# Both parts of an operand form as one 512-column moving operand in a seven-product feed-forward input projection

## The chip, the core and the metric

The kernel runs on one core of a Trainium2 chip. The metric is the device time of one execution in microseconds (us), as the median over several executions. The engines are named as the profile names them: PE is TensorE's matmul side and PEld its weight loads, DVE is VectorE, ACT is ScalarE, POOL is GpSimd, SP is SyncE, which here only issues DMAs.

## The reference

One layer of a causal decoder: a mixer sublayer, a memory cross-attention sublayer, a SwiGLU feed-forward sublayer and a final norm, for 512 tokens of width 1024. The change lies in the first half of the feed-forward sublayer:

```python
D_MODEL = 1024; SEQ = 512; FFN_HIDDEN = 2816

def rms_norm(x, g):
    xf = x.astype(jnp.float32)
    var = jnp.mean(xf * xf, axis=-1, keepdims=True)
    return (xf * lax.rsqrt(var + EPS) * g.astype(jnp.float32)).astype(x.dtype)

# ... mixer and memory sublayers leave the residual stream x ...
hf = rms_norm(x, norm_ffn[l])
gate, up = jnp.split(hf @ w_ffn_in[l], 2, axis=-1)      # (512, 1024) @ (1024, 5632)
x = x + (jax.nn.silu(gate) * up) @ w_ffn_out[l]
# final: rms_norm(x, norm_final)
```

All arrays are float32.

## The kernel before

Activations lie transposed: model dimension on the 128 partitions, the 512 tokens along the free dimension. A float32 operand is not multiplied as one number: it is split into a rounded part ("hi", made by an ACT cast to fp32r) and the rest ("lo", made by a DVE subtract), and a product is the sum of three matmuls, hi·hi, hi·lo and lo·hi.

The feed-forward input is computed in blocks. The hidden width 2816 makes NF = 22 blocks of 128 gate rows and 128 up rows. In each block m the product of a 2x2 arrangement of weights (gate and up rows by even and odd 128-row chunks of the model dimension) with a 2x2 arrangement of activations (even and odd chunks by two halves of HS = 256 tokens) is made from seven products instead of eight. `forms_of` builds the seven activation forms for each of the KP = 4 pairs of chunks; each is 256 columns wide and is split into hi and lo. The weight forms come per block: two are loaded as they are (`wg`), two come out of a DMA that adds to what is already in the tile (`ws`, first loaded by SP at L763, then added to by POOL's DMA at L768), one is loaded as it is (`a22`, L767), and two are sums made by an engine (`s2`, L779). Each weight form is then cast and subtracted (`ffn_form`, L792, L793, L801, L802).

`product(ps, m, i)` issues product i: for each of the four chunk pairs three matmuls of 256 columns (L811), 12 in all, and 84 per block. They go into the left half of a PSUM bank. A block uses three banks: z collects products 0, 3, 4 and 5 as a running sum, v takes product 1, y takes product 2 and then 6. `reads` and `second` copy or add what the running sums hold after certain products (ACT copies at L831, DVE adds at L833, L836, L841), `evict` scales the gate by the norm factor (L848, DVE), takes silu (L850, ACT) and multiplies with the negated up half (L855, DVE), which gives the block's activation `act`.

The order around it is written out by hand. `uses` lists all products; in the steady part a block is the seven uses (m,3), (m+1,0), (m,4), (m+1,1), (m,5), (m+1,2), (m,6). For use n the loop issues its matmuls, its reads, then the weight form of use n + AHEAD (6 ahead), then the raw weights of use n + 8, then the norm and eviction steps of other blocks. On PE, ACT and DVE instructions stand in exactly that order (`manual_schedule`); POOL and SP are left to the scheduler and carry in this stage only the DMA issues (POOL also made one sum ahead of the loop). Weight tiles come from rotating buffers, so a load waits until the form made from the tile's previous content is done. The last stage, the output projection (matmuls at L155 to L157 into `f`), begins when the loop ends.

Of the kernel before, what the change touches and what calls it, by code (L numbers as in the profile page):

```python
# [40 lines left out]
def hybrid_layer(ctx: ExitStack, tc: tile.TileContext, xT_d, memT_d, cols_d, wv_d, win_d,  # L41
# [576 lines left out]
    def forms_of(xe, xo):  # L618

        b11, b12, b21, b22 = xe[:, :HS], xe[:, HS:], xo[:, :HS], xo[:, HS:]
        c, d = f(unit("c1")), f(unit("c2"))
        n1, t3, n2, t4 = c[:, :HS], c[:, HS:], d[:, :HS], d[:, HS:]
        nc.vector.tensor_tensor(out=n1, in0=b11, in1=b12, op=ALU.subtract)
        nc.vector.tensor_tensor(out=t3, in0=b22, in1=b12, op=ALU.subtract)  # L626
        nc.vector.scalar_tensor_tensor(out=n2, in0=n1, scalar=-1.0, in1=b22, op0=ALU.mult,
                                       op1=ALU.subtract)
        nc.vector.scalar_tensor_tensor(out=t4, in0=n2, scalar=-1.0, in1=b21, op0=ALU.mult,
                                       op1=ALU.subtract)  # L630
        u = unit("xf")
# [3 lines left out]
        a, b = slice(0, HS), slice(HS, S)  # L635
        return [(u[:, a], u[:, b]), (oh[:, a], ol[:, a]), (ch[:, a], cl[:, a]),
                (dh[:, a], dl[:, a]), (ch[:, b], cl[:, b]), (dh[:, b], dl[:, b]),
                (oh[:, b], ol[:, b])]

    def residual(w_dram, act, old, gain, pairs=False):  # L640

# [107 lines left out]
    KP = KD // 2  # L749
    SCALED = 3  # L750
    AHEAD = 6
    SUM_AHEAD = 2
    FORM_TAGS = "wh", "wl"

    raws, pairs = {}, {}

    def ffn_load(m):

        a = wfi_d[m].rearrange("p (i c) -> p i c", i=4)
# [6 lines left out]
        a22 = fpool.tile([P, 512], F32, tag="w2", name=nm("a22"), bufs=4)  # L766
        nc.sync.dma_start(a22, a[:, 3, :])  # L767
        nc.gpsimd.dma_start(s13, a[:, 0:4:3, :], accum_op=ALU.add)  # L768
        pairs[m] = wg
        raws[m] = [wg[:, 0, :], wg[:, 1, :], s13[:, 1, :], None, s13[:, 0, :], a22, None]  # L770

    def ffn_raw(m, i, eng=nc.vector):
        if m not in raws:
            ffn_load(m)
        w = raws[m]
        if w[i] is None:
            w[i] = fpool.tile([P, 512], F32, tag="w2", name=nm("s2"), bufs=4)
            a, b = (w[2], w[0]) if i == 3 else (w[3], w[1])
            eng.tensor_tensor(out=w[i], in0=a, in1=b, op=ALU.add)  # L779
        return w[i]  # L780

    wforms, made = {}, [0]

    def ffn_form(m, i):

        if (m, i) in wforms:
            return
        if i == 0:
            ffn_raw(m, i)
            pair = pairs[m]  # L790
            hi, lo = (wpool.tile([P, 2, 512], F32R, tag=t, name=nm("wf")) for t in FORM_TAGS)
            nc.scalar.copy(hi, pair)  # L792
            nc.vector.tensor_tensor(out=lo, in0=pair, in1=f(hi), op=ALU.subtract)  # L793
            for j in range(2):
                wforms[m, j] = hi[:, j, :], lo[:, j, :]
            return
        raw = ffn_raw(m, i)
# [3 lines left out]
        nc.scalar.copy(hi, raw)  # L801
        nc.vector.tensor_tensor(out=lo, in0=raw, in1=f(hi), op=ALU.subtract)  # L802

    def product(ps, m, i, ks=range(KP)):

        w = wforms[m, i]
        for k in ks:
            hi, lo = (w[j][:, k * P:(k + 1) * P] for j in range(2))
            xh, xl = x2f[k][i]
            for j, (a, b) in enumerate(((hi, xh), (hi, xl), (lo, xh))):  # L810
                nc.tensor.matmul(ps[:, :HS], a, b, start=i < 3 and k == 0 and j == 0,  # L811
                                 stop=k == KP - 1 and j == 2, skip_group_check=True)

    banks, act, silus, stts = {}, {}, [], []

    def bank_of(m, i):
        if i == 0:
            banks[m] = {"z": ztile("z"), "s": tmp("sa"), "t": tmp("sb")}
        elif i == 1:
            banks[m]["v"] = mmtile("v")  # L820
            banks[m]["g"] = tmp("fg")
        elif i == 2:
            banks[m]["y"] = otile("y")
        return banks[m]["zvyzzzy"[i]]

    def reads(m, i):

        b = banks[m]
        z, s, t = b["z"][:, :HS], b["s"], b["t"]
        if i in (0, 3, 4):  # L830
            nc.scalar.copy((s[:, :HS], None, None, s[:, HS:], t[:, :HS])[i], z)  # L831
        elif i == 1:
            nc.vector.tensor_tensor(out=b["g"][:, :HS], in0=b["v"][:, :HS], in1=s[:, :HS],  # L833
                                    op=ALU.add)
        elif i == 6:
            nc.vector.tensor_tensor(out=b["g"][:, HS:], in0=b["y"][:, :HS], in1=s[:, HS:],  # L836
                                    op=ALU.add)

    def second(m):
        b = banks[m]  # L840
        nc.vector.tensor_tensor(out=b["t"][:, HS:], in0=b["y"][:, :HS], in1=b["t"][:, :HS],  # L841
                                op=ALU.add)

    def evict(m, part):
        b = banks[m]
        g = b["g"]
        if part == 0:
            nc.vector.tensor_tensor(out=g, in0=g, in1=r2b[0], op=ALU.mult)  # L848
        elif part == 1:
            silus.append(nc.scalar.activation(g, g, AF.Silu))  # L850
        else:
            a = act[m] = f(unit("act"))
            for half, u in enumerate((b["z"][:, :HS], b["t"][:, HS:])):
                sl = slice(half * HS, (half + 1) * HS)
                stts.append(nc.vector.scalar_tensor_tensor(out=a[:, sl], in0=u, scalar=-1.0,  # L855
                                                           in1=g[:, sl], op0=ALU.mult,
                                                           op1=ALU.mult))

    uses = [(0, 0), (0, 1), (0, 2)]
    for m in range(NF):  # L860
        if m < NF - 2:
            uses += [(m, 3), (m + 1, 0), (m, 4), (m + 1, 1), (m, 5), (m + 1, 2), (m, 6)]
        elif m == NF - 2:
            uses += [(m, 3), (m + 1, 0), (m, 4), (m + 1, 1), (m + 1, 2), (m + 1, 3), (m, 5),
                     (m + 1, 4), (m, 6), (m + 1, 5), (m + 1, 6)]
    actp = {}
    r2b = [None]

# [10 lines left out]
    for n in range(AHEAD + SUM_AHEAD):  # L879
        ffn_raw(*uses[n], nc.gpsimd)  # L880
    for n in range(AHEAD):
        ffn_form(*uses[n])
    with tc.manual_schedule(engines={mybir.EngineType.PE, mybir.EngineType.Activation,
                                     mybir.EngineType.DVE}):
        ahead = uses[:3] + [(1, 0)]
        for m, i in ahead:
            product(bank_of(m, i), m, i, range(KP - 1 - m))
# [2 lines left out]
        for n, (m, i) in enumerate(uses):  # L890
            if (m, i) == (1, 0):
                product(banks[m]["z"], m, i, range(KP - 2, KP))
            elif n > 2:
                product(bank_of(m, i), m, i)
            if i == 4:
                reads(m, i)
            elif i == 5 and m == NF - 1:
                reads(m, i)
                second(m)
            else:  # L900
                if i == 1 and m > 0:
                    second(m - 1)
                reads(m, i)
            if n + AHEAD < len(uses):
                ffn_form(*uses[n + AHEAD])
            if n + AHEAD + SUM_AHEAD < len(uses):
                ffn_raw(*uses[n + AHEAD + SUM_AHEAD])
            if (m, i) == (0, 5):
                mean2 = squares_mean(acc2, TT)
            if (m, i) == (0, 6):  # L910
                r2b[0] = mean2[1]("r0b", bank=mmtile, keep=rms)
            if (m, i) == (1, 6):
# [7 lines left out]
            if i == 0 and m > 1:  # L920
                evict(m - 2, 0)
            elif i == 4 and 0 < m < NF - 1:
# [5 lines left out]
            if (m, i) == (NF - 2, 6):  # L928
                evict(m, 0)
                evict(m, 1)  # L930
            if (m, i) == (NF - 1, 5):
                evict(NF - 2, 2)
        evict(NF - 1, 0)
        evict(NF - 1, 1)
# [169 lines left out]
```

## Time and profile before

| | |
|---|---|
| median of 3 runs | 863.53 us (863.06 to 864.0) |
| the profiled execution, its own time | 864.6 us |
| its span, first to last instruction | 861.8 us |
| PE busy | 854.1 us, 99% of the span |
| DVE busy | 586.9 us, 68% |
| ACT busy | 440.2 us, 51% |
| POOL busy | 69.2 us, 8% |
| granted TensorE clock, mean | 0.999 |

In the rows of the profile, `L811 PE MATMUL z<-xdh,wf 128*128 128x256` means: source line 811, engine, operation, tile written, tiles read, shape. In the views of groups the figures behind the bar are the busy microseconds of the group, the mean nanoseconds of one instruction, and the idle time of the engine just before, with what ended it. In a timeline the two leading figures are the start and the duration in microseconds; brackets hold idle time of the engine before the instruction and what released it. Durations of neighbouring instructions on one engine overlap a little, so the step from start to start is shorter than the duration.

### The profile page before, as it was taken

How to read it: one execution, taken by the hardware profiler on the slowest of the kernel's cores; microseconds unless marked ns; L12 is line 12 of the kernel's file. 1: busy time of each engine (PE TensorE's matmuls, PEld its weight loads, DVE VectorE, ACT ScalarE, POOL GpSimd, SP SyncE). 2: the span in 40 equal slices, each digit the busy share in tenths (PEclk: the TensorE clock that was granted, in tenths of full speed). 3: DMA queues.
4: the chain of work that ended last, by engine and by line, in shares of the span. 5: the costliest groups of instructions: out<-in, count | busy, mean ns of one | idle time of the engine just before them, and what ended most of it. 6: DMA issues, size and time to landing. Idle time of an engine off the chain costs nothing.

```text
span 861.8 us, 12717 instructions
## 1 busy us (share of the span) xinstructions
PE 854.1 (99%) x4932; PEld 750.9 (87%) x4932; DVE 586.9 (68%) x964; ACT 440.2 (51%) x774; POOL 69.2 (8%) x105
## 2 busy tenths in 40 slices
PE   9999999999999999999999999999999999999997
PEld 7887888888888898888888889999999999888897
DVE  8768898986555466555555879888887778533334
ACT  7476787675333244443444656555445556322335
POOL 2022131111000000000000101111111100000002
PEclk9999999999999999999999999999999999999999
DMA  8432331228333345422111427777677763322202
GB/s 294 131 101 86 106 115 50 74 84 266 115 110 110 98 159 188 154 97 93 57 49 49 135 50 199 188 182 178 175 190 192 188 151 122 123 98 98 74 1 97
DMA packets 42347, 108.32 MB, mean 126 GB/s; under 512 B 4144, under 2 KB 8240, under 8 KB 42288
## 3 DMA queue, kind: packets, MB, share of 16 engines
q1 hardware_dynamic: 36016, 95.70, 32.8%
q0 software_dynamic: 5984, 11.54, 8.2%
q8 instruction: 38, 0.62, 0.3%
q10 hardware_dynamic: 288, 0.29, 0.1%
q14 instruction: 21, 0.17, 0.1%
HBM read 104.36 MB, written 2.10 MB: 124 GB/s over the span
## 4 chain that ended last, share of the span: by engine, by line
PE 98%; DVE 1%; ACT 0%; issue 0%; POOL 0%; DVEq 0%; POOLq 0%
PE z L811 15%; PE y L811 7%; PE pr L155 7%; PE pr L157 7%; PE pr L156 7%; PE f L157 5%; PE f L155 5%; PE f L156 5%; PE v L811 4%; PE r L155 3%; PE r L156 3%; PE r L157 3%; PE v L261 3%; PE mq L155 2%; PE mq L157 2%; PE mq L156 2%
## 5 line engine op out<-in xcount | busy, mean ns | idle before, releaser
L150 ACT CAST wh<-wr 128x1024 fp32r<-128x1024 f32 x106 | 111.0, 1051 | 215.2 <-issue 98.6
L151 DVE TENSOR_TENSOR wl<-wr,wh 128x1024 fp32r<-128x1024 f32 x106 | 129.4, 1223 | 100.0 <-ACT wh L150 100.0
L155 PE MATMUL pr<-xgh,wh 128*128 128x512 f32 x288 | 112.5, 391 | 0.0
L156 PE MATMUL pr<-xgl,wh 128*128 128x512 f32 x288 | 112.2, 390 | 0.0
L157 PE MATMUL pr<-xgh,wl 128*128 128x512 f32 x288 | 112.2, 390 | 0.0
L156 PE MATMUL f<-actl,wh 128*128 128x512 f32 (+1 forms) x208 | 74.2, 357 | 0.0
L155 PE MATMUL f<-acth,wh 128*128 128x512 f32 (+1 forms) x208 | 74.2, 357 | 0.0
L157 PE MATMUL f<-acth,wl 128*128 128x512 f32 (+1 forms) x208 | 74.0, 356 | 0.0
L811 PE MATMUL z<-xdh,wf 128*128 128x256 f32 x352 | 70.3, 283 | 0.0
L768 POOL DMA_DIRECT2D ws<-in_w_ffn_in_dram x22 | 26.6, 1208 | 468.7 <-DVE c L626 267.3
L157 PEld LDWEIGHTS pr<-xgh,wl 128*128 128x128 f32 x288 | 54.1, 188 | 11.4
L156 PEld LDWEIGHTS pr<-xgl,wh 128*128 128x128 f32 x288 | 54.1, 188 | 10.8
L155 PEld LDWEIGHTS pr<-xgh,wh 128*128 128x128 f32 x288 | 54.1, 188 | 10.8
L811 PEld LDWEIGHTS z<-xdh,wf 128*128 128x128 f32 x352 | 58.0, 192 | 0.0
L831 ACT COPY sa<-z 128x256 f32<-128x256 f32 x44 | 16.4, 373 | 77.8 <-PE z L811 77.8
L811 PE MATMUL z<-xdl,wf 128*128 128x256 f32 x176 | 49.8, 283 | 0.0
L802 DVE TENSOR_TENSOR wf<-s,wf 128x512 fp32r<-128x512 f32 x44 | 30.3, 690 | 20.9 <-ACT wf L801 19.8
L155 PEld LDWEIGHTS f<-acth,wh 128*128 128x128 f32 x208 | 39.3, 189 | 5.7
L157 PEld LDWEIGHTS f<-acth,wl 128*128 128x128 f32 x208 | 39.3, 189 | 5.6
L156 PEld LDWEIGHTS f<-actl,wh 128*128 128x128 f32 x208 | 39.3, 189 | 5.6
L811 PE MATMUL y<-xch,wf 128*128 128x256 f32 x176 | 35.5, 283 | 0.0
L811 PE MATMUL v<-xoh,wf 128*128 128x256 f32 x176 | 35.5, 283 | 0.0
(290 smaller groups left out, 2158.9 us busy)
## 6 DMA issues: line engine op xcount, KB each, us to landing
wr<-in_w_in_dram SPq DMA_DIRECT2D x36, 512.0 KB, 3.3
ws<-in_w_ffn_in_dram SPq DMA_DIRECT2D x22, 512.0 KB, 3.8
wg<-in_w_ffn_in_dram SPq DMA_DIRECT2D x22, 512.0 KB, 4.2
ws<-in_w_ffn_in_dram POOLq DMA_DIRECT2D x22, 512.0 KB, 5.7
wr<-in_w_ffn_out_dram SPq DMA_DIRECT2D x22, 512.0 KB, 3.2
a<-in_w_ffn_in_dram SPq DMA_DIRECT2D x22, 256.0 KB, 4.6
wr<-in_w_branch_dram SPq DMA_DIRECT2D x8, 512.0 KB, 3.2
wr<-in_w_mem_k_dram SPq DMA_DIRECT2D x8, 512.0 KB, 3.2
```

What stands on the lines that cost most here:

```text
L150: after(nc.scalar.copy(h2, raw), lead[-1:])
L151: lows.append(nc.vector.tensor_tensor(out=l2, in0=raw, in1=f(h2), op=ALU.subtract))
L155: nc.tensor.matmul(ps, a[0], b[0], start=start, stop=False, **kw)
L156: nc.tensor.matmul(ps, a[0], b[1], start=False, stop=False, **kw)
L157: nc.tensor.matmul(ps, a[1], b[0], start=False, stop=stop, **kw)
L261: nc.tensor.matmul(vps[t], xg[k][a][:, sl], wv[k][b], start=k == 0 and (a, b) == (0, 0), stop=k == KD - 1 and a == 1)
L768: nc.gpsimd.dma_start(s13, a[:, 0:4:3, :], accum_op=ALU.add)
L802: nc.vector.tensor_tensor(out=lo, in0=raw, in1=f(hi), op=ALU.subtract)
L811: nc.tensor.matmul(ps[:, :HS], a, b, start=i < 3 and k == 0 and j == 0, stop=k == KP - 1 and j == 2, skip_group_check=True)
L831: nc.scalar.copy((s[:, :HS], None, None, s[:, HS:], t[:, :HS])[i], z)
```

## The change

- `forms_of` writes hi and lo of an activation form side by side into one 512-column tile, for all seven forms (before: one form so, the other six as halves of three 512-wide splits).
- `product` issues two matmuls per chunk pair in place of three: the hi weights against the 512 columns [hi | lo], and the lo weights against the 256 columns hi. The left half of a bank now holds hi·hi + lo·hi, the right half hi·lo, and the two halves have to be added.
- The reads widen from 256 to 512 columns (both bank halves), and `fold` adds the halves in SBUF, on POOL in all blocks but the last (three folds of 256 columns per block). For product 5 ACT copies the right half and DVE adds the left.
- The two weight sums per block go from DVE to POOL, and so does the scaling by the norm factor. The final multiply becomes one of 512 columns instead of two of 256.
- POOL's order is now written by hand too. `LEADS` fixes how far ahead the loads (12 uses), the adding DMA (9), the `a22` load (11) and the sums (8 and 9) are issued. In steady blocks POOL's order is: fold of `act`, fold of the gate's left half, sum for form 6, sum for form 3, fold of the gate's right half, scaling, adding DMA.
- The scaling of `x2T` by `rms` is spread over every second block.

```diff
-        u = unit("xf")
-        nc.scalar.copy(u[:, :HS], b11)
-        nc.vector.tensor_tensor(out=u[:, HS:], in0=b11, in1=f(u[:, :HS]), op=ALU.subtract)
-        (oh, ol), (ch, cl), (dh, dl) = split(xo, "xo"), split(c, "xc"), split(d, "xd")
...
+        for raw in (b11, xo[:, :HS], n1, n2, t3, t4, xo[:, HS:]):
+            u = unit("xf")
+            nc.scalar.copy(u[:, :HS], raw)
+            nc.vector.tensor_tensor(out=u[:, HS:], in0=raw, in1=f(u[:, :HS]), op=ALU.subtract)
+            got.append(u)
...
+    def ffn_accumulate(m):
+        nc.gpsimd.dma_start(sums13[m], ffn_blocks(m)[:, 0:4:3, :], accum_op=ALU.add)
+    def ffn_last(m):
+        a22 = raws[m][5] = fpool.tile([P, 512], F32, tag="w2", name=nm("a22"), bufs=4)
+        nc.sync.dma_start(a22, ffn_blocks(m)[:, 3, :])
+    def ffn_sum(m, i):
...
+        nc.gpsimd.tensor_tensor(out=w[i], in0=a, in1=b, op=ALU.add)
...
-            for j, (a, b) in enumerate(((hi, xh), (hi, xl), (lo, xh))):
-                nc.tensor.matmul(ps[:, :HS], a, b, start=i < 3 and k == 0 and j == 0,
-                                 stop=k == KP - 1 and j == 2, skip_group_check=True)
+            nc.tensor.matmul(ps, hi[:, sl], x, start=i < 3 and k == 0, stop=False,
+                             skip_group_check=True)
+            nc.tensor.matmul(ps[:, :HS], lo[:, sl], x[:, :HS], start=False, stop=k == KP - 1,
+                             skip_group_check=True)
...
+    def fold(m, out, src):
+        eng = nc.vector if m == NF - 1 else nc.gpsimd
+        eng.tensor_tensor(out=out, in0=src[:, :HS], in1=src[:, HS:], op=ALU.add)
...
         if i in (0, 3, 4):
-            nc.scalar.copy((s[:, :HS], None, None, s[:, HS:], t[:, :HS])[i], z)
+            nc.scalar.copy({0: g, 3: b.get("s"), 4: b.get("t")}[i], z)
         elif i == 1:
-            nc.vector.tensor_tensor(out=b["g"][:, :HS], in0=b["v"][:, :HS], in1=s[:, :HS],
-                                    op=ALU.add)
+            nc.vector.tensor_tensor(out=g, in0=b["v"], in1=g, op=ALU.add)
+            fold(m, g[:, :HS], g)
+        elif i == 5:
+            a = act[m][:, :HS]
+            nc.scalar.copy(a, z[:, HS:])
+            nc.vector.tensor_tensor(out=a, in0=z[:, :HS], in1=a, op=ALU.add)
         elif i == 6:
...
+            nc.vector.tensor_tensor(out=s, in0=b["y"], in1=s, op=ALU.add)
+            fold(m, g[:, HS:], s)
     def second(m):
...
+        nc.vector.tensor_tensor(out=t, in0=b["y"], in1=t, op=ALU.add)
+        act[m] = f(unit("act"))
+        fold(m, act[m][:, HS:], t)
     def evict(m, part):
...
-            nc.vector.tensor_tensor(out=g, in0=g, in1=r2b[0], op=ALU.mult)
+            eng = nc.vector if m == NF - 1 else nc.gpsimd
+            eng.tensor_tensor(out=g, in0=g, in1=r2b[0], op=ALU.mult)
...
+            stts.append(nc.vector.scalar_tensor_tensor(out=act[m], in0=act[m], scalar=-1.0, in1=g,
+                                                       op0=ALU.mult, op1=ALU.mult))
...
+    LEADS = ((12, 0, ffn_load), (9, 0, ffn_accumulate), (11, 5, ffn_last),
+             (8, 6, lambda m: ffn_sum(m, 6)), (9, 3, lambda m: ffn_sum(m, 3)))
...
-                                     mybir.EngineType.DVE}):
+                                     mybir.EngineType.DVE, mybir.EngineType.Pool}):
...
-            if i == 3 and 2 <= m < 2 + KD:
-                x = x2T[m - 2]
+            if i == 3 and m % 2 == 0 and 2 <= m < 2 + 2 * KD:
+                x = x2T[m // 2 - 1]
```

More of the change, by code (lines that the diff above doesn't have):

```diff
@@ L751, in hybrid_layer, with ffn_blocks @@
     AHEAD = 6
-    SUM_AHEAD = 2
     FORM_TAGS = "wh", "wl"
-    raws, pairs = {}, {}
+    raws, pairs, sums13 = {}, {}, {}
+    def ffn_blocks(m):
+        return wfi_d[m].rearrange("p (i c) -> p i c", i=4)
     def ffn_load(m):
-        a = wfi_d[m].rearrange("p (i c) -> p i c", i=4)
+        a = ffn_blocks(m)
         s13, wg = ((fpool, "wg") if (m % 3, t) in ((1, "ws"), (2, "wg")) else (wpool, "wr")
@@ L765, in ffn_load @@
         nc.sync.dma_start(wg, a[:, 0:2, :])
[L766 to L774, printed above, removed]
-        w = raws[m]
[L776 to L780, printed above, removed]
+        pairs[m], sums13[m] = wg, s13
+        raws[m] = [wg[:, 0, :], wg[:, 1, :], s13[:, 1, :], None, s13[:, 0, :], None, None]
+    def ffn_accumulate(m):
[4 more added lines that the diff above has]
+    def ffn_sum(m, i):
+        w = raws[m]
+        w[i] = fpool.tile([P, 512], F32, tag="w2", name=nm("s2"), bufs=4)
+        a, b = (w[2], w[0]) if i == 3 else (w[3], w[1])
+        nc.gpsimd.tensor_tensor(out=w[i], in0=a, in1=b, op=ALU.add)
     wforms, made = {}, [0]
@@ L788, in ffn_form @@
         if i == 0:
-            ffn_raw(m, i)
             pair = pairs[m]
@@ L851, in evict @@
         else:
[L852 to L857, printed above, removed]
+            stts.append(nc.vector.scalar_tensor_tensor(out=act[m], in0=act[m], scalar=-1.0, in1=g,
+                                                       op0=ALU.mult, op1=ALU.mult))
     uses = [(0, 0), (0, 1), (0, 2)]
@@ L865, in hybrid_layer, with ffn_prepare @@
                      (m + 1, 4), (m, 6), (m + 1, 5), (m + 1, 6)]
+    LEADS = ((12, 0, ffn_load), (9, 0, ffn_accumulate), (11, 5, ffn_last),
+             (8, 6, lambda m: ffn_sum(m, 6)), (9, 3, lambda m: ffn_sum(m, 3)))
+    def ffn_prepare(n, only=None):
+        for lead, i, do in LEADS:
+            if 0 <= n + lead < len(uses) and uses[n + lead][1] == i and (only is None or
+                                                                         (do == ffn_accumulate)
+                                                                         == only):
+                do(uses[n + lead][0])
     actp = {}
@@ L877, in act_parts @@
         after(nc.vector.tensor_tensor(out=lo, in0=a, in1=f(hi), op=ALU.subtract), behind)
-    for n in range(AHEAD + SUM_AHEAD):
-        ffn_raw(*uses[n], nc.gpsimd)
+    for n in range(-12, 0):
+        ffn_prepare(n)
     for n in range(AHEAD):
@@ L894, in hybrid_layer @@
                 product(bank_of(m, i), m, i)
[L895 to L898, printed above, removed]
+            if i == 1 and m > 0:
+                second(m - 1)
+            if (m, i) == (NF - 1, 5):
                 second(m)
[L900 to L903, printed above, removed]
+            ffn_prepare(n, False)
+            reads(m, i)
             if n + AHEAD < len(uses):
                 ffn_form(*uses[n + AHEAD])
-            if n + AHEAD + SUM_AHEAD < len(uses):
-                ffn_raw(*uses[n + AHEAD + SUM_AHEAD])
+            if i == 6 and m < NF - 1 and r2b[0] is not None:
+                evict(m, 0)
+            ffn_prepare(n, True)
             if (m, i) == (0, 5):
@@ L911, in hybrid_layer @@
                 r2b[0] = mean2[1]("r0b", bank=mmtile, keep=rms)
+                evict(0, 0)
             if (m, i) == (1, 6):
```

39 lines of the change are left out of this document (16 added, 23 removed).

## The prediction

> **What bounds the kernel now.** I read the busy shares first, then the shares of the chain that ended last, both on the page.
>
> ```profile
> PE 854.1 (99%) x4932; PEld 750.9 (87%) x4932; DVE 586.9 (68%) x964; ACT 440.2 (51%) x774; POOL 69.2 (8%) x105
> ...
> PE 98%; DVE 1%; ACT 0%; issue 0%; POOL 0%; DVEq 0%; POOLq 0%
> ```
>
> PE sets the end almost everywhere. The stage that changes was read next: the busy time in the steady stretch 540 to 700 us (columns: length, then PE, PEld, DVE, ACT, POOL busy with counts, clock, DMA share, GB/s), and the chain in order of time around one block.
>
> ```profile
> 540.00:700.00 160.00, 160.00 (x1336) 160.00 (x1335) 130.84 (x231) 83.17 (x159) 19.25 (x16) 1.00 0.72 184
> ```
>
> ```profile
> 592.08 2.88 PE y L811 x24
> 594.96 4.32 PE z L811 x36
> ...
> 602.16 2.88 PE y L811 x24
> ```
>
> The same piece of the chain comes back after 602.16 - 592.08 = 10.08 us: that is a block, 84 matmuls at 0.120 us. PE never waits in it and the clock is full. There are 160 / 10.08 = 15.9 blocks in the stretch, so a block takes 130.84 / 15.9 = 8.2 us of DVE and 5.2 of ACT. Both have slack, and the timelines of the two engines show it: DVE and ACT are idle for want of each other or of PE.
>
> ```profile
> 598.80 0.69 DVE L802 TENSOR_TENSOR wf<-s,wf 128x512 fp32r<-128x512 f32 x1
> 599.41 0.68 DVE L848 TENSOR_TENSOR fg<-fg,r0b 128x512 f32<-128x512 f32 x1
> 600.73 1.23 DVE L793 TENSOR_TENSOR wf<-wg,wf 128x1024 fp32r<-128x1024 f32 x1 [0.63 <-ACT wf L792]
> 601.87 0.42 DVE L841 TENSOR_TENSOR sb<-y,sb 128x256 f32<-128x256 f32 x1
> 602.21 0.41 DVE L833 TENSOR_TENSOR fg<-v,sa 128x256 f32<-128x256 f32 x1
> ```
>
> ```profile
> 606.52 0.37 ACT L831 COPY sa<-z 128x256 f32<-128x256 f32 x1 [3.65 <-PE z L811]
> ```
>
> **PE's part.** PE's timeline, first and last row of five consecutive 256-column matmuls, and of nine consecutive 512-column ones in the output projection:
>
> ```profile
> 620.36 0.28 PE L811 MATMUL v<-xoh,wf 128*128 128x256 f32 x1
> ...
> 620.84 0.28 PE L811 MATMUL z<-xdl,wf 128*128 128x256 f32 x1
> ```
>
> ```profile
> 779.53 0.39 PE L156 MATMUL f<-actl,wh 128*128 128x512 f32 x1
> ...
> 781.35 0.39 PE L155 MATMUL f<-acth,wh 128*128 128x512 f32 x1
> ```
>
> Start to start is 0.48 / 4 = 0.120 us for 256 columns and 1.82 / 8 = 0.2275 for 512. Twice 256 columns costs 0.240, so each merged pair saves 0.0125 us. There are 22 blocks x 7 products x 4 chunk pairs = 616 pairs: 7.7 us. A block on PE becomes 28 x 0.2275 + 28 x 0.120 = 9.73 us, 0.35 less. The columns that are streamed stay the same; only a fixed share per matmul is saved. The Trainium skill, "TensorE: Matmul & The Clock Gate", section "Wait — 56ns, not 53.3ns?", speaks against that gain: a warm matmul costs its columns at 2.4 GHz plus about 2.5 ns, which would make the whole saving 616 x 2.5 ns = 1.5 us (an estimate from that page). The two rows do not agree with it: they leave 0.0125 us per matmul, five times as much.
>
> **DVE's part.** In the five rows of DVE above durations overlap by some 0.07 us, so I count steps from start to start: 0.61 for 512 columns (598.80 to 599.41), 1.14 for 1024 (600.73 to 601.87), 0.34 for 256 (601.87 to 602.21). Off DVE go two sums and the scaling, 3 x 0.61. On come the wider reads: three of 0.61 for three of 0.34, and a new one of 0.34; the final multiply stays at about 0.61. A block after: five form subtracts and the multiply 6 x 0.61 = 3.66, the pair 1.14, the `x2T` scaling 0.61 in 8 of 22 blocks = 0.22, which is 5.02 us with both inputs in SBUF; and 3 x 0.61 + 0.34 = 2.17 us with one input in PSUM. 7.2 of 9.73: by itself DVE gets lighter.
>
> **ACT's part.**
>
> ```profile
> L801 ACT CAST wf<-s 128x512 fp32r<-128x512 f32 x28 | 17.4, 622 | 0.0
> ...
> L831 ACT COPY sa<-z 128x256 f32<-128x256 f32 x28 | 10.4, 372 | 58.4 <-PE z L811 58.4
> ```
>
> Three copies widen by 0.25 us (0.622 for 0.372) and one of 0.37 is added: 5.2 + 1.1 = 6.3 us of 9.73, hidden.
>
> **POOL's part, where the question lies.** POOL gets three 512-column two-input operations and three of 256 per block, beside its DMA issue. Before, this stage has none of these. Rows of the nearest kind stand at the kernel's end, in the attention stage and in the stretch 560 to 700:
>
> ```profile
> L1039 POOL TENSOR_TENSOR yg<-yg,rf x4: 1262/1277/1287, 849.5 to 853.3; 128x512 f32<-128x512 f32 x4
> ```
>
> ```profile
> L768 POOL DMA_DIRECT2D ws<-in_w_ffn_in_dram x14 | 16.8, 1203 | 124.3 <-DMA ws<-in_w_ffn_in_dram 114.7 <-DVE wf L802 9.6
> ```
>
> ```profile
> 56.22 0.73 POOL L502 TENSOR_TENSOR accm<-accm,mk 128x256 f32<-128x256 f32 x1
> ...
> 98.38 1.27 POOL L502 TENSOR_TENSOR accm<-accm,mk 128x256 f32<-128x256 f32 x1
> ...
> 116.72 1.61 POOL L502 TENSOR_TENSOR accm<-accm,mk 128x256 f32<-128x256 f32 x1 [2.98 <-ACT mk L497]
> 118.41 2.25 POOL L502 TENSOR_TENSOR accm<-accm,mk 128x256 f32<-128x256 f32 x1
> ```
>
> By undisturbed durations POOL's block is 3 x 1.28 + 3 x 0.73 + 1.20 = 7.2 us of 9.73, and it would fit. But the same 256-column add took from 0.73 to 2.25 us. DVE's timeline beside the long ones:
>
> ```profile
> 98.36 0.68 DVE L463 TENSOR_TENSOR al<-a,ah 128x512 fp32r<-128x512 f32 x1
> 98.98 1.08 DVE L376 TENSOR_TENSOR l<-e,l 128x384 fp32r<-128x384 f32 x1
> ...
> 101.48 0.56 DVE L376 TENSOR_TENSOR l<-e,l 128x384 fp32r<-128x384 f32 x1 [0.82 <-ACT l L375]
> ```
>
> ```profile
> 117.65 0.68 DVE L294 SCALAR_TENSOR_TENSOR qk<-pr,r0b 128x512 f32<-128x512 f32 x1
> 118.25 1.22 DVE L151 TENSOR_TENSOR wl<-wr,wh 128x1024 fp32r<-128x1024 f32 x1
> 119.38 0.68 DVE L170 TENSOR_TENSOR qkl<-qk,qkh 128x512 fp32r<-128x512 f32 x1
> ```
>
> The add of 118.41 ended at 120.66, 0.60 us after the second of two DVE subtracts (118.25 and 119.38, the last ending at 120.06); both read two SBUF tensors. The add of 98.38 ended at 99.65, 0.61 after DVE's at 98.36 was over, and the DVE operation that followed took 1.08 instead of 0.56: it stood 0.52 for POOL. So these two kinds of instruction do not run beside each other; one stands still. The Trainium skill, "SBUF — State Buffer", section "Who interferes with whom", says so as an exclusive lock that a DVE instruction with two SBUF inputs and a reading GpSimd instruction take in turn, whoever issues first. The trace agrees on the lock but not on the turn: the subtract of 119.38 started a microsecond after the add and still went ahead. A DVE read from PSUM is not concerned (the one of 117.65, whose first input is PSUM, and the add of 116.72 were under way together and both ended at 118.33).
>
> The price of a POOL operation on the shared path is thus 0.52 to 0.60 us for 256 columns, and 0.55 more for 512 (1.28 - 0.73): 1.07 to 1.15. A block needs 3 x 0.52 + 3 x 1.07 = 4.77 to 5.25 us of POOL there, and 5.02 of DVE: 9.8 to 10.3 us, when PE's block is 9.73. The path would have to be taken without a break.
>
> It has breaks. The block in DVE's order, with POOL's operation that is ready beside it: pair subtract 1.14; read of y 0.61 (POOL's next input is this read's output, so nothing beside it); read of v 0.61 (fold of `act` beside it); subtract, multiply 2 x 0.61; second fold, with the short read of z beside it; subtract 0.61; sum for form 6, with the read of y beside it; subtract 0.61; sum for form 3; subtract 0.61; third fold; subtract 0.61 and 0.22 of scaling; POOL's scaling; then the DMA issue, beside which the next block begins. DVE's pieces are 1.14 + 2 x 0.61 + 6 x 0.61 + 0.22 = 6.24; POOL's that stand by themselves are two folds and three of 512, 2 x 0.52 + 3 x 1.07 = 4.25 to 2 x 0.60 + 3 x 1.15 = 4.65. Together 10.5 to 10.9, middle 10.7. I take the middle, since rows bear out both ends equally.
>
> PE cannot run ahead of this for long: product 6 adds onto the y bank that DVE must have read before, and that read stands behind the pair subtract in DVE's order; and ACT's copies of z stand in one queue with casts that now wait for POOL's sums. Behind ACT's waiting cast stand the copies that free z, and behind POOL's waiting fold stand the sums; DVE's subtracts wait for both.
>
> **The rest, each bounded.** The adding DMA now stands in POOL's order with six operations behind it. SP's plain load has 3.9 us to landing:
>
> ```profile
> ws<-in_w_ffn_in_dram SPq DMA_DIRECT2D x14, 512.0 KB, 3.9
> ```
>
> Its tile is free (last form made) most of a block before the adding DMA's turn, so I count nothing; if loads came later than a block, POOL's six would wait up to the missing time, 1 us per block as a high end. SP's queue only gets the same loads in another order. `forms_of` costs ACT six more short casts for three fewer long ones per call, 7 x 0.37 - 0.37 - 3 x 0.62 = 0.4 us, and DVE 7 x 0.34 - 0.34 - 3 x 0.61 = 0.2; the residual's matmuls hide it but for the last of four calls, at most 0.4 us, not below nothing since no instruction goes. First and last block: no crowding on POOL, PE's 0.35 each is gained.
>
> **Sum.** 20 blocks x (10.7 - 10.08) = +12.4, two outer blocks -0.7: +11.7 us. On the profiled execution, 861.8 us of span and 2.8 around it, that is 876.3; its time is 1.1 above the median of the runs, so against the median 875. With 10.5 it is +7.7 (871). With 10.9 and half of a 0.62 us cast uncovered per block, 11.2: +21.7 (885). The likeliest case's own range is 871 to 885.
>
> **Rivals.**
> - The other side: POOL's operations fall into DVE's gaps and PSUM reads, and PE stays the bound at 9.73: 863.5 - 7.7 = 855.8. For it: PE waits nowhere now, DVE falls to 7.2 us and each engine alone has 2.5 us to spare. It decides at 9.73 - 5.02 = 4.71 us of POOL per block: with less than that, or if POOL's and DVE's operations of these forms do run together, the sum fits. Against it: the 4.77 above, and that is the low end. Chance 0.27.
> - The path is the bound but filled without a break, 9.8 to 10.2 us per block: -0.28 to +0.12 x 20 - 0.7, that is 857 to 865. Against it: folds whose input appears only with the read that would cover them. Chance 0.08, half of it under -0.2%.
> - PE saves nothing and nothing else binds: a weight load goes with each matmul, and if a 512-column one among 256-column ones takes 2 x 0.120, the block stays 10.08: 863.5. By the page's 2.5 ns it would be 862.0. Against both: 0.2275 in the projection. Chance 0.02.
> - The adding DMA comes late at 1 us per block with all of POOL behind it: 863.5 + 22 = 885. Against it: 3.9 us to landing. Chance 0.03.
>
> **How the numbers follow.** The shared path as the bound has 0.60. 0.2% of this time is 1.7 us, about what a measurement of this kernel tells from no change. Faster: 0.27 + 0.04 = 0.31. Same: 0.02 + 0.03 = 0.05. Slower: 0.60 + 0.03 + 0.01 = 0.64. The range reaches from PE's bound, 855, to 887 (the likeliest case's 885 and 0.1 us more per block); what it leaves out is a steeper pile-up.
>
> **What would show it.** In the steady stretch: a chain that comes back after 10.5 to 10.9 us with DVE, POOL and ACT in it, POOL adds far above 1.28 us and 0.73 us, some DVE subtracts above 0.69, PE waiting for y or z. It is wrong if PE stays unbroken at 9.73 us per block; PE's step is wrong if a 512 and a 256 together take other than 0.3475 us; the lock's step is wrong if POOL's adds keep 1.28 beside DVE subtracts.

## The result and the profile after

The changed kernel takes 886.13 us (median of 4 runs, 885.52 to 887.02), the kernel before 863.76 on the same chip (863.06 to 864.74): a ratio of 1.0259, 95% interval 1.0241 to 1.0277. The profiled execution has a span of 884.4 us and took 886.14, so 22.6 us more of span than before, where 11.7 were forecast.

I read the profile after in the same order: busy shares, shares of the chain, and the busy time of the steady stretch 540 to 700 us (length, then PE, PEld, DVE, ACT, POOL, clock, DMA share, GB/s).

```profile
PE 858.4 (97%) x4316; PEld 718.4 (81%) x4316; DVE 645.2 (73%) x915; ACT 461.7 (52%) x808; POOL 237.8 (27%) x232
...
PE 72%; POOL 14%; DMA 10%; DVE 3%; ACT 1%; issue 1%; DVEq 0%; POOLq 0%; ACTq 0%
```

```profile
540.00:700.00 160.00, 148.30 (x817) 124.59 (x816) 159.97 (x171) 91.47 (x162) 133.46 (x103) 1.00 0.65 167
```

PE has gone from 160.00 of 160 us to 148.30, and DVE from 130.84 to 159.97. Yet DVE executes less: 171 instructions instead of 231. A busy DVE here is partly a standing one, since an instruction counts as busy while it stands. The DVE groups of the stretch 560 to 720 (count, busy us, mean ns of one) show which kinds have grown, and POOL's groups the other side:

```profile
L803 DVE TENSOR_TENSOR wf<-s,wf 128x512 fp32r<-128x512 f32 x30 | 36.7, 1245 | 0.0
L803 DVE TENSOR_TENSOR wf<-ws,wf 128x512 fp32r<-128x512 f32 x29 | 30.4, 1047 | 0.0
L803 DVE TENSOR_TENSOR wf<-a,wf 128x512 fp32r<-128x512 f32 x15 | 21.7, 1446 | 0.0
L868 DVE SCALAR_TENSOR_TENSOR act<-act,fg 128x512 f32<-128x512 f32 x15 | 18.3, 1223 | 0.0
...
L940 DVE TENSOR_TENSOR x<-x,rms 128x512 f32<-128x512 f32 x7 | 12.4, 1778 | 0.0
...
L842 DVE TENSOR_TENSOR fg<-v,fg 128x512 f32<-128x512 f32 x14 | 9.4, 674 | 0.0
```

```profile
L782 POOL TENSOR_TENSOR s<-ws,wg 128x512 f32<-128x512 f32 x15 | 26.2, 1745 | 0.0
...
L832 POOL TENSOR_TENSOR fg<-fg 128x256 f32<-128x256 f32 x15 | 17.7, 1178 | 0.0
...
L832 POOL TENSOR_TENSOR act<-sb 128x256 f32<-128x256 f32 x14 | 10.2, 731 | 22.2 <-DVE sb L856 22.2
```

Every 512-column DVE group with two inputs in SBUF is far above its undisturbed 0.68 us (the 1024-column pair subtract, which falls where POOL waits for DVE's next read, keeps 1.21); the add that reads a PSUM bank (`fg<-v,fg`) keeps 0.674. On POOL the fold that falls beside such a PSUM read (`act<-sb`) keeps 0.731; the other folds take 1.18 and the sums 1.75 instead of 1.28. Per block, two `s` subtracts, two `ws` subtracts, one `a` subtract, one multiply and half an `x2T` scaling give 2 x 0.56 + 2 x 0.36 + 0.76 + 0.54 + 0.55 = 3.7 us of standing. With 7.2 us of DVE's own work that is 10.9. The waits of the stage (total us, times, longest) and the start of a block in the two timelines show how it reaches PE, which waits for the y bank until DVE has read it:

```profile
ACT wf L802 <- DMA ws<-in_w_ffn_in_dram: 64.3, 18, 4.0
...
PEld y L810 <- DVE sb L856: 19.1, 18, 2.3
PE y L810 <- DVE sb L856: 13.4, 18, 2.0
```

```profile
604.39 1.44 DVE L803 TENSOR_TENSOR wf<-a,wf 128x512 fp32r<-128x512 f32 x1
605.76 0.68 DVE L850 TENSOR_TENSOR sa<-y,sa 128x512 f32<-128x512 f32 x1
606.36 1.18 DVE L803 TENSOR_TENSOR wf<-ws,wf 128x512 fp32r<-128x512 f32 x1
```

```profile
603.55 1.74 POOL L782 TENSOR_TENSOR s<-s,wg 128x512 f32<-128x512 f32 x1
605.25 1.74 POOL L782 TENSOR_TENSOR s<-ws,wg 128x512 f32<-128x512 f32 x1
```

POOL's first sum ends at 605.29, and DVE's subtract that began beside it ends at 605.83, 0.54 us later: it did nearly all of its work after the sum. POOL's next sum, begun at 605.25 while that subtract was still at work, takes 1.74 us and ends at 606.99; the `ws` subtract begun at 606.36 again ends 0.55 after it. The two engines take turns. Here the turn goes to whichever began first, as the Trainium skill's "SBUF — State Buffer", section "Who interferes with whom", has it.

The chain of waits comes back after alternately 10.55 and 11.19 us; the longer piece follows an `x2T` scaling, which DVE began at 608.60:

```profile
599.22 4.37 DMA ws<-in_w_ffn_in_dram
...
609.77 4.98 DMA ws<-in_w_ffn_in_dram
...
620.96 4.37 DMA ws<-in_w_ffn_in_dram
```

The mean is 10.87, at the top of the forecast 10.5 to 10.9. But these lines also offer another cause: the chain names the adding DMA in every block, and ACT's casts wait 64 us for it. Against that speaks the 0.0 of idle time in every DVE group above: no cast was late for DVE in this stretch. The experiments had to tell the causes apart.

### The profile page after: what moved, and what is told of

The parts are those of the page before. It is cut to its first block, busy times and chain, and to the rows that moved or that the text cites. A ratio compares the mean times of both kernels' runs of the same rounds, so it can differ in the third digit from the quotient of the medians.

```text
span 884.4 us, 11674 instructions
## 1 busy us (share of the span) xinstructions
PE 858.4 (97%) x4316; PEld 718.4 (81%) x4316; DVE 645.2 (73%) x915; ACT 461.7 (52%) x808; POOL 237.8 (27%) x232
## 4 chain that ended last, share of the span: by engine, by line
PE 72%; POOL 14%; DMA 10%; DVE 3%; ACT 1%; issue 1%; DVEq 0%; POOLq 0%; ACTq 0%
DMA ws<-in_w_ffn_in_dram 10%; PE pr L155 7%; POOL s L782 7%; PE pr L156 7%; PE pr L157 7%; PE f L155 4%; PE f L156 4%; PE f L157 4%; POOL fg L864 4%; PE r L156 3%; PE r L157 3%; PE r L155 3%; POOL fg L832 3%; PE v L261 3%; PE mq L157 2%; PE mq L155 2%
## 5 line engine op out<-in xcount | busy, mean ns | idle before, releaser
L810 PE MATMUL z<-xf,wf 128*128 128x512 f32 x352 | 128.4, 403 | 3.1 <-ACT sa L840 3.1
L812 PE MATMUL z<-xf,wf 128*128 128x256 f32 x352 | 99.0, 281 | 0.0
L810 PEld LDWEIGHTS z<-xf,wf 128*128 128x128 f32 x352 | 66.6, 189 | 21.8 <-ACT sa L840 5.5
L810 PE MATMUL y<-xf,wf 128*128 128x512 f32 x176 | 66.0, 409 | 13.4 <-DVE sb L856 13.4
L812 PEld LDWEIGHTS z<-xf,wf 128*128 128x128 f32 x352 | 67.0, 190 | 0.1
L802 ACT CAST wf<-ws 128x512 fp32r<-128x512 f32 x44 | 27.0, 615 | 72.1 <-DMA ws<-in_w_ffn_in_dram 64.3
L155 PEld LDWEIGHTS pr<-xgh,wh 128*128 128x128 f32 x288 | 54.1, 188 | 10.9
L810 PEld LDWEIGHTS y<-xf,wf 128*128 128x128 f32 x176 | 33.3, 189 | 26.5 <-DVE sb L856 19.1
L803 DVE TENSOR_TENSOR wf<-s,wf 128x512 fp32r<-128x512 f32 x44 | 51.4, 1187 | 0.7 <-ACT wf L802 0.6
L812 PE MATMUL y<-xf,wf 128*128 128x256 f32 x176 | 49.4, 281 | 0.0
L803 DVE TENSOR_TENSOR wf<-ws,wf 128x512 fp32r<-128x512 f32 x44 | 45.1, 1026 | 1.5 <-ACT wf L802 1.5
```

Of the source, the lines that this page charges most:

```text
L155: nc.tensor.matmul(ps, a[0], b[0], start=start, stop=False, **kw)
L810: nc.tensor.matmul(ps, hi[:, sl], x, start=i < 3 and k == 0, stop=False, skip_group_check=True)
L812: nc.tensor.matmul(ps[:, :HS], lo[:, sl], x[:, :HS], start=False, stop=k == KP - 1, skip_group_check=True)
```

## The experiments

Theory A: DVE and POOL on their shared path are the bound. B: the adding DMA, now last in POOL's order, with ACT's wait for it, closes the loop. C: DVE is simply overloaded. Ratios are to the kernel before on the same chip, with 95% intervals.

**POOL only writes.** Sums, folds and scaling on POOL become pairs of memsets into the same tiles, so these values are left out of the result; the order and the DMAs stay.

```diff
-        nc.gpsimd.tensor_tensor(out=w[i], in0=a, in1=b, op=ALU.add)
+        for _ in range(2):
+            nc.gpsimd.memset(w[i], 0.5)
...
+                nc.gpsimd.memset(out, 0.5)
...
+                    nc.gpsimd.memset(g, 0.5)
```

> The change with POOL's sums, folds and scaling in all blocks but the last replaced by pairs of memsets of the same outputs, in the same places of POOL's order: POOL writes SBUF and reads none, and the values are not the sums. POOL's block is then about 6 x (0.5 to 1.0) + 1.2 = 6 us. Theory A: DVE's 512-column subtracts fall back from 1.0 to 1.45 us to 0.69, DVE's block to 7.2, PE is the bound at 9.77: 856 to 858 us. Rival B: the adding DMA still stands last in POOL's order and ACT still waits for it: over 870.

860.42 us, 0.9957 (0.9942 to 0.9972): 25.7 us below the changed kernel. Its steady stretch, a DVE and a POOL group:

```profile
540.00:700.00 160.00, 160.00 (x907) 138.85 (x906) 119.72 (x185) 102.27 (x179) 96.64 (x208) 1.00 0.74 186
```

```profile
L804 DVE TENSOR_TENSOR wf<-s,wf 128x512 fp32r<-128x512 f32 x32 | 22.1, 692 | 20.7 <-ACT wf L803 20.0
```

```profile
L783 POOL MEMSET s<- 128x512 f32 x66 | 33.7, 524 | 2.6 <-DVE wf L804 0.7
```

POOL is still busy for 96.64 us of 160, with the same order and the same adding DMA, but DVE's subtracts are back at 0.692 and PE is unbroken. What makes DVE stand is that POOL reads SBUF. The Trainium skill, "SBUF — State Buffer", section "Who interferes with whom", says that too: DVE's instructions with two SBUF inputs contend with a GpSimd instruction that reads SBUF, not with one that only writes it; the 0.692 agrees. PE alone gives its step here: 907 matmuls in 160 us are 0.353 us per pair, not 0.3475, and a block of 28 pairs takes 9.89 us, not the 9.77 behind A's 856 to 858. Memsets also shorten POOL's part of the order and wait for no inputs, so this run alone doesn't clear B.

**Everything back on DVE.** Sums (but for the last two blocks' own), folds and scaling go to DVE; POOL keeps the DMA.

```diff
-        nc.gpsimd.tensor_tensor(out=w[i], in0=a, in1=b, op=ALU.add)
+        (nc.vector if 0 in banks and m < NF - 2 else nc.gpsimd).tensor_tensor(
+            out=w[i], in0=a, in1=b, op=ALU.add)
...
-        eng = nc.vector if m == NF - 1 else nc.gpsimd
+        eng = nc.vector
```

> The change with the sums (but two of the last blocks), folds and scaling on DVE instead of POOL. Theory A (the shared path: DVE's operations with two SBUF inputs and POOL's stand for each other, and DVE with the time it stands, 7.2 + 3.7 us, is the bound at 10.87 us per block): DVE's own work grows by 2 x 0.61 + 0.61 + 3 x 0.34 = 2.9 us to 10.05 us per block, but it stands for nothing: 10.05 to 10.3 us per block, 864 to 870 us, although DVE gets more to do. Rival B (the adding DMA stands last in POOL's order and lands 5.6 us after; ACT's cast waits for it, and this loop over two blocks sets the period): POOL is empty, so about the same, 864 to 870. Rival C (DVE is simply overloaded, whoever makes it wait): slower than 886.

874.43 us, 1.0121 (1.0106 to 1.0136): DVE has some 3 us more work per block, and the kernel is 11.7 us faster than with POOL's help. The subtracts are undisturbed, and DVE is nearly full with work of its own:

```profile
540.00:700.00 160.00, 154.47 (x860) 131.28 (x859) 158.37 (x271) 97.00 (x170) 19.24 (x16) 1.00 0.70 178
```

```profile
L804 DVE TENSOR_TENSOR wf<-s,wf 128x512 fp32r<-128x512 f32 x30 | 19.9, 685 | 0.0
```

C falls as a cause of the changed kernel's time: its own 7.2 us do not fill DVE. My number missed by 4 us, because I had left out that the block with the `x2T` scaling is 0.6 us longer (blocks alternate between 10.07 and 10.67 us) and that DVE has more to do at the ends of the stage: two blocks at its start take 13.32 and 11.85 us, where the kernel before has 10.67 and 10.00.

**Only the sums back on DVE**, by the first of the two edits above.

> The change with only the two weight sums per block back on DVE (but two of the last blocks); folds and scaling stay on POOL. Theory A: DVE's own work 7.2 + 1.2 = 8.4 us, and it stands for two folds and the scaling (the third fold lies beside a PSUM read), 2 x 0.52 + 1.07 = 2.1: 10.5 us per block, 886 - 20 x 0.35 = about 879. Rival B: POOL's order is 3.4 us shorter, the adding DMA goes out early, PE becomes the bound at 9.77 us per block: about 860 or less. Rival C: slower than 886.

884.32 us, 1.0235 (1.0218 to 1.0252), 5 us above what A expected, and far from B's 860. The two sums cost DVE 1.2 us of work and took back as much standing, no more:

```profile
L804 DVE TENSOR_TENSOR wf<-s,wf 128x512 fp32r<-128x512 f32 x30 | 36.7, 1245 | 0.0
...
L804 DVE TENSOR_TENSOR wf<-a,wf 128x512 fp32r<-128x512 f32 x15 | 10.2, 680 | 0.0
```

```profile
POOL fg L833 <- DVE sa L851: 68.5, 19, 7.4
```

POOL, with a shorter queue, now waits 68.5 us in the stage for DVE's reads, and the time hardly moves. That alone does not refute B: the DMA still stands behind folds that wait for these reads, and ACT still waits 54.8 us for it. But DVE is busy for 159.94 of the 160 us here, with nothing idle. The `a` subtract is free, while the `s` subtracts still stand for a fold and the scaling. Standing was 3.7 us with five reading operations in DVE's way and is 2.4 with three, so a sum had cost 0.6 us, not the 1.1 that A had put on it; the rest of it ran beside PSUM reads, as the timeline above shows.

**The adding DMA ahead of the sums** in POOL's order.

```diff
-    LEADS = ((12, 0, ffn_load), (9, 0, ffn_accumulate), (11, 5, ffn_last),
+    LEADS = ((12, 0, ffn_load), (11, 0, ffn_accumulate), (11, 5, ffn_last),
```

> The change with the adding DMA two uses earlier in POOL's order (lead 11 for 9), ahead of the two sums instead of behind the scaling; all else as it is. Theory A: ACT no longer waits for that DMA, but DVE is full with its own work and the time it stands: 884 to 888 us, 10.8 to 10.9 us per block. Rival B: the DMA leaves the loop, at least 1 us per block goes: 866 or less.

914.89 us, 1.0585 (1.0569 to 1.0601): both theories' numbers missed. ACT's wait for the DMA, 64.3 us before, is gone from the list of waits, and the kernel is 29 us slower. DVE and POOL at one place of a block:

```profile
604.71 3.44 DVE L803 TENSOR_TENSOR wf<-a,wf 128x512 fp32r<-128x512 f32 x1
```

```profile
604.62 1.72 POOL L782 TENSOR_TENSOR s<-s,wg 128x512 f32<-128x512 f32 x1
605.86 1.73 POOL L782 TENSOR_TENSOR s<-ws,wg 128x512 f32<-128x512 f32 x1
```

The two sums now follow each other without a turn for DVE, and a subtract of 0.68 us stands through both. The turn does not go to whichever began first here: the second sum, begun at 605.86, goes ahead of the subtract begun at 604.71. The order of POOL's work has changed along with the wait, but DVE accounts for the blocks, which take 12.08 or 12.67 us: its own 7.2 us and 5.2 of standing (2.8 for the `a` subtract, 2 x 0.56 and 2 x 0.11 for the others, 0.54 and 0.55 as before), and it is busy for 159.97 of the 160 us. The granted clock is 0.96 in this stretch, but DVE has no idle time in which it waits for PE. So B is out for the steady blocks: the wait for the DMA is slack there. And the price of an operation on the shared path depends on what stands beside it.

**Narrow matmuls in the changed kernel.** PE's wide matmul is cut into two of 256 columns, one per half of the bank. With the start flag now set on both halves, the sums are no longer those of the changed kernel.

```diff
-            nc.tensor.matmul(ps, hi[:, sl], x, start=i < 3 and k == 0, stop=False,
-                              skip_group_check=True)
+            for j in range(2):
+                js = slice(j * HS, (j + 1) * HS)
+                nc.tensor.matmul(ps[:, js], hi[:, sl], x[:, js], start=i < 3 and k == 0,
+                                 stop=False, skip_group_check=True)
```

> The changed kernel with the wide matmul cut back into two of 256 columns, each into its half of the bank; everything behind TensorE as in the changed kernel. Theory A (DVE and GpSimd on their shared path are the bound, blocks of 10.87 us): TensorE's work in a block goes back from 9.89 to 10.08 us and stays below the path's 10.87, so the time is that of the changed kernel, 886 us within 1.5. Rival P (part of the loss is TensorE's, because a wide matmul holds or frees a bank in coarser pieces): the time moves by more than that, down to 882 or below if the coarse pieces cost, up to 890 (616 pairs x 0.007 us) if TensorE's saving was worth its full size.

886.04 us, 1.0263 (1.0248 to 1.0279), the changed kernel's time to 0.1 us. What the change gives PE is worth nothing in it; the loss is behind PE.

**POOL's sums and scaling in the kernel before.** (The expectation's "three sums and the scaling" are two sums and the scaling, three operations; its arithmetic counts them so.)

```diff
-    def ffn_raw(m, i, eng=nc.vector):
+    def ffn_raw(m, i, eng=nc.gpsimd):
...
-            nc.vector.tensor_tensor(out=g, in0=g, in1=r2b[0], op=ALU.mult)
+            (nc.vector if m > NF - 3 else nc.gpsimd).tensor_tensor(out=g, in0=g, in1=r2b[0], op=ALU.mult)
...
-                                     mybir.EngineType.DVE}):
+                                     mybir.EngineType.DVE, mybir.EngineType.Pool}):
```

> The kernel before, with its narrow matmuls and narrow reads, but with the three sums and (except in the last two blocks) the scaling of a block on GpSimd as in the changed kernel. Theory A: DVE's own work of 8.2 us per block loses 3 x 0.61 and gains some 3 x 1.1 us of standing for GpSimd, 9.7 us, below TensorE's 10.08: the time stays at 862 to 867, while the subtracts beside the sums grow from 0.69 to over 1.0 us on the mean and DVE is busy for more than 145 us of the 160 in the steady stretch. Rival F (the price is only paid where GpSimd's operations wait on DVE's and DVE's on them, that is through the folds): the subtracts keep 0.69 to 0.75 us, and DVE's busy time falls to about 105 of 160. Rival C (the sums on GpSimd are dear by themselves): 10 us or more above the kernel before.

865.42 us, 1.002 (1.0011 to 1.0029): within A's 862 to 867. The standing is there, without any fold or wide read, but smaller than expected:

```profile
540.00:700.00 160.00, 160.00 (x1335) 159.99 (x1334) 127.63 (x184) 83.63 (x160) 92.18 (x65) 1.00 0.74 184
```

```profile
L802 DVE TENSOR_TENSOR wf<-s,wf 128x512 fp32r<-128x512 f32 x32 | 33.3, 1041 | 25.9 <-ACT wf L801 25.3
L802 DVE TENSOR_TENSOR wf<-ws,wf 128x512 fp32r<-128x512 f32 x32 | 28.1, 879 | 0.0
```

About 1.4 us of standing per block (2 x 0.36 + 2 x 0.19 + 0.06 + 0.19 of a multiply), where I had put 3.3. DVE comes out at 127.63 us of 160, where over 145 was expected, hardly less than the 130.84 before: three operations fewer gain it next to nothing. PE still covers that, so the time barely moves.

**One fold on POOL.** Of all that the change moved, only the `act` fold beside the PSUM read stays on POOL.

```diff
-    def fold(m, out, src):
-        eng = nc.vector if m == NF - 1 else nc.gpsimd
+    def fold(m, out, src, eng=nc.vector):
...
-        fold(m, act[m][:, HS:], t)
+        fold(m, act[m][:, HS:], t, nc.vector if m == NF - 1 else nc.gpsimd)
```

> The changed kernel with all sums, scalings and folds on DVE but one: the fold into the second half of the act tile, which stood beside DVE's read of a PSUM bank and took 0.73 us, stays on GpSimd. Theory A: DVE loses 0.34 to 0.45 us per block against the version with everything on DVE (874.4 us) and gains no standing: 20 x 0.35 to 0.45 = 7 to 9 us less, 865 to 868; its subtracts keep 0.69 us. Rival: any fold on GpSimd costs a hand-over that eats this, 873 to 876, or the lock finds it in its new place, subtracts above 0.9 us and a time above 876.

867.83 us, 1.0051 (1.0037 to 1.0065): 6.6 us faster than with this fold on DVE (6.0 by the ratios, since the chips differ), inside A's range and close to its upper end.

```profile
L832 POOL TENSOR_TENSOR act<-sb 128x256 f32<-128x256 f32 x16 | 11.7, 730 | 128.5 <-DVE sb L856 128.5
```

```profile
L804 DVE TENSOR_TENSOR wf<-s,wf 128x512 fp32r<-128x512 f32 x32 | 21.1, 684 | 0.0
```

The fold keeps its 0.73 us and the subtracts their 0.684. POOL's help is free where DVE reads a PSUM bank at that time, and only there. The loop still comes back after 9.72 or 10.32 us, DVE being full.

**Fewer merged products.** The pair of 0.353 us is a real gain, so the last two kernels look for a version that keeps it without filling DVE. The kernel before, with products 1, 2 and 6 merged; DVE adds the halves in two reads of 256 columns, nothing goes to POOL.

```diff
+    MERGED = 1, 2, 6
...
+            if i in MERGED:
+                nc.tensor.matmul(ps, hi, x, start=i < 3 and k == 0, stop=False,
+                                 skip_group_check=True)
+                nc.tensor.matmul(ps[:, :HS], lo, x[:, :HS], start=False, stop=k == KP - 1,
+                                 skip_group_check=True)
+                continue
...
+    def add_both(out, bank, other):
+        for part in (bank[:, :HS], bank[:, HS:]):
+            nc.vector.tensor_tensor(out=out, in0=part, in1=other, op=ALU.add)
+            other = out
```

> The kernel before with only products 1, 2 and 6 merged (banks v and y, whose halves DVE adds in two reads of 256 columns, PSUM plus SBUF), the other four products as before, and nothing moved to GpSimd. Theory A: DVE goes from 8.2 to about 9.3 us per block, below TensorE's; no operation shares a path with GpSimd; TensorE gains 12 pairs x 22 blocks x 0.007 us = 1.8 us, so 861 to 863. Rival H (a merged bank is held longer by its two reads, and TensorE waits for it): TensorE stands once or twice a block, 865 us or more. If a pair saved 0.0125 us as first forecast, 860.5.

863.9 us, 1.0005 (0.9996 to 1.0014), no difference, where A expected 861 to 863. The inner blocks do come back after 10.00 us, but the first ones have lost as much: PE's piece of 36 matmuls on z begins at 546.29 us, in the kernel before at 544.56. At the last such piece, 716.28 against 715.92, the inner blocks have won most of that back.

**The same in blocks 4 to 18 alone.**

```diff
-    MERGED = 1, 2, 6
+    MERGED, INNER = (1, 2, 6), range(4, NF - 3)
...
-            if i in MERGED:
+            if i in MERGED and m in INNER:
```

> The kernel before with products 1, 2 and 6 merged in blocks 4 to 18 alone; the four first and three last blocks as in the kernel before. Theory O (the version that merges them in all 22 blocks came out level because the blocks at both ends, where DVE has other work and TensorE waits for it, give back what the inner ones gain): 15 blocks x 12 pairs x 0.007 us = 1.2 us less than the kernel before, 862.2 within 0.7. Rival (the merged blocks only look shorter, and the gain is given back by a wait further on, in the output projection): 863.4 or more, with a later last matmul of the feed-forward stage made up or not.

862.09 us, 0.9979 (0.997 to 0.9988), where 862.2 was expected: the one version with nothing left out that beats both kernels, the kernel before by 1.8 us.

```profile
540.00:700.00 160.00, 160.00 (x1169) 151.82 (x1168) 146.76 (x275) 84.08 (x161) 19.25 (x16) 1.00 0.74 184
```

PE is unbroken at full clock, with DVE at 146.76 of 160.

## Why the prediction was right, and where its sum was off

Right, by its own steps: the time came within the range, on the side held likelier. It is higher than the forecast 875 by 11 us, 1 us above the likeliest case's own range and 0.9 us below the end of the whole range, 887. That the range still held it is partly luck, since 10.2 of the 22.6 us came up where the sum had put -0.7.

- **The shared path sets the block.** Forecast 10.5 to 10.9 us, measured 10.87 in the steady stretch, and the signs that were named appeared: subtracts above 0.69, sums above 1.28, PE waiting for y. Only the chain runs over POOL and its DMA, not over DVE and ACT. Shown by taking POOL's reads away (PE unbroken) and by putting POOL's work on DVE (faster). After the last `x2T` scaling a block takes 10.51. From DVE's pair subtract at 545.65 to the one at 729.42 there are 17 blocks of 10.81 us on the mean, 12.4 us more than 17 in the kernel before (540.25 to 711.61): as much as the forecast had put on 20.
- **The price of a POOL operation** held as a lock that makes one of the two engines stand; as a sum of fixed prices it did not: a sum cost 0.6 us in one order, some 1.4 where two stood in a row ahead of one subtract (3.44 - 0.68 = 2.8 for the two), and the `act` fold nothing beside a PSUM read.
- **PE's step was mis-sized.** 0.2275 + 0.120 came from runs of equal matmuls; alternating, the pair takes 0.353. The saving is 616 x 0.007 = 4.3 us, not 7.7. In the changed kernel it counts for nothing (the cut-back matmuls change 0.1 us), so the outer blocks' -0.7 could not come. By the Trainium skill, "TensorE: Matmul & The Clock Gate", section "Wait — 56ns, not 53.3ns?", it would be 1.5 us (the estimate of the prediction); the measured step lies between the two.
- **The outer blocks were the step that failed.** I had them gain 0.7 us. First and last matmul of the stage, before and after, PE's waits at its ends, and DVE's pair subtract in the first blocks, before and after:

```profile
509.07 0.40 PE L811 MATMUL z<-xf,wf 128*128 128x256 f32 x2
...
733.12 0.28 PE L811 MATMUL y<-xoh,wf 128*128 128x256 f32 x1
```

```profile
509.19 0.39 PE L810 MATMUL z<-xf,wf 128*128 128x512 f32 x1
...
525.84 0.50 PE L197 MATMUL varb<-accl,mean_r 128*128 128x512 f32 x1 [1.11 <-DVE accl L181]
535.41 0.50 PE L810 MATMUL y<-xf,wf 128*128 128x512 f32 x1 [0.76 <-DVE sb L856]
547.52 0.50 PE L810 MATMUL y<-xf,wf 128*128 128x512 f32 x1 [1.95 <-DVE sb L856]
...
747.25 0.79 PE L810 MATMUL z<-xf,wf 128*128 128x512 f32 x1 [1.44 <-ACT sa L840]
...
754.60 0.28 PE L812 MATMUL y<-xf,wf 128*128 128x256 f32 x1
```

```profile
519.58 1.23 DVE L793 TENSOR_TENSOR wf<-wg,wf 128x1024 fp32r<-128x1024 f32 x1 [0.82 <-ACT wf L792]
...
530.25 1.22 DVE L793 TENSOR_TENSOR wf<-wg,wf 128x1024 fp32r<-128x1024 f32 x1
...
540.25 1.23 DVE L793 TENSOR_TENSOR wf<-wg,wf 128x1024 fp32r<-128x1024 f32 x1
```

```profile
519.93 1.23 DVE L794 TENSOR_TENSOR wf<-wg,wf 128x1024 fp32r<-128x1024 f32 x1 [1.08 <-ACT wf L793]
...
533.55 1.21 DVE L794 TENSOR_TENSOR wf<-wg,wf 128x1024 fp32r<-128x1024 f32 x1
...
545.65 1.21 DVE L794 TENSOR_TENSOR wf<-wg,wf 128x1024 fp32r<-128x1024 f32 x1
```

  The stage grew by 245.41 - 224.05 = 21.4 us. The 17 blocks are 12.4 of it; 9.0 lie at its ends, and 1.2 more come outside the stage. At the start, DVE's two blocks take 25.72 us instead of 20.67, 5.1 more. In the kernel before DVE was busy for 19.97 of these 20.67 us, since it also has the norm's work there; it had no room for standing. With POOL only writing the two blocks take 20.91, and with everything on DVE 25.17. The version with the three merged products shows the same kind of loss there without any POOL work, and leaving the outer blocks out removes it. Behind the pair subtract of 729.42 the stage loses another 3.7 us. Part of that is the granted clock, 0.91 between 735 and 755 us: five pairs of matmuls from 747.25 on take 3.55 us where 5 x 0.353 would be 1.8. How the rest of the 3.7 divides was not tried.
- **The adding DMA**, counted at nothing: ACT does wait for it, 64.3 us in all, but in the steady blocks the wait is slack. Near the end it is not: DVE once stands 1.47 us for a cast that waited for this DMA. The rival that gave 885, near the measured time, had the right size from the wrong cause; moving the DMA forward made it 914.89.
- **ACT** stayed hidden, as counted: 91.47 of 160 us.

Together: 12.4 in 17 blocks where 12.4 were forecast for 20, 9.0 instead of -0.7 at the ends, 1.2 outside, which is 22.6 for 11.7.

## What to carry to other kernels

In this kernel, moving work from DVE to GpSimd was free where DVE at that moment read a PSUM bank. Elsewhere part of GpSimd's time came back as standing of DVE, 0.6 to 1.4 us for a sum that costs DVE 0.61, and the order of the two queues set the price along with the amount of work. One input in SBUF instead of two was no protection for every instruction: a one-input operation of the norm took 0.42 us in the kernel before (first row) and 0.96 in the changed one (second row), beside a fold on POOL (third row).

```profile
536.63 0.42 DVE L913 TENSOR_SCALAR eps_sq<-rms 128x512 f32<-128x512 f32 x1
```

```profile
541.27 0.96 DVE L935 TENSOR_SCALAR eps_sq<-rms 128x512 f32<-128x512 f32 x1
```

```profile
540.75 1.19 POOL L832 TENSOR_TENSOR fg<-sa 128x256 f32<-128x256 f32 x1
```

Read a "full" engine by its mean durations: here DVE was 100% busy, and a third of that it stood. A change that gains a little on the bounding engine and loads the next one may pay in part, where that engine has room, when the whole of it doesn't: here three of seven products, in the inner blocks alone.

## What the runs showed of the hardware

A 512-column fp32r matmul followed by one of 256 columns costs 0.353 us, 5 ns more than the two cost in runs of their own kind (0.2275 and 0.120). DVE instructions stood for up to 2.8 us (3.44 for 0.68) behind two GpSimd reads in a row. A GpSimd that only writes, busy for 96.64 us of 160 with its DMA issues, cost DVE's two-input subtracts nothing; a one-input cast of the norm took 0.64 us beside it, 0.42 in the kernel before.
